# A re-planned start for a tuned RMSNorm and matmul kernel: weights first, two tiles transposed by the DMA crossbar, the next tiles fetched earlier

## The chip, the cores and the metric

One core of one Trainium2 chip. Times are device microseconds (us) of that core; one execution of a kernel is one time. The span is the profile's time from the first to the last instruction, some 2 us less than the measured time. A run and the kernel before are compared on the same chip in the same rounds.

Words used below: SBUF is the on-chip memory of the core, PSUM the one into which TensorE writes. An eviction copies a finished result from PSUM to SBUF. A crossbar transpose is a DMA that reads a tile from SBUF and writes it back transposed. A transfer lands when the profile shows it complete; its time to landing is counted from its issue. The granted clock is the share of its full speed at which TensorE ran, as the profile records it.

## The reference, cut to what matters

```python
# x: (8, 1024, 768), w_qkv: (768, 2304), all float32
rms = np.sqrt(np.mean(x ** 2, axis=-1, keepdims=True) + eps)
return np.matmul(x / rms * gamma, w_qkv)
```

x is 8192 rows, 64 tiles of 128 rows. For each tile the kernel does 6 blocks of K times 2304 columns: 24 matmuls of 512 columns and 6 of 256.

## The kernel before

The whole program is a list of (planned time, operation), sorted by time. Each engine gets its operations in that order and waits, in order, for what each one needs. The first six tiles, "the head", follow a hand-made plan while the weights arrive; from tile 6 on each tile repeats one pattern.

```python
    def load_w(c): ...                       # SyncE: float32 piece of the weights, in 2 KB or 1 KB rows
    def conv(c, ko, eng): ...                # gamma * w -> bf16, on VectorE, ScalarE or GpSimd
    def cast(t, eng="DVE"): ...              # x tile -> bf16
    def tr(t):                               # six transposes on TensorE, into PSUM
        PT[t] = psum.tile([P, KO, P], bf16, name="pm")
        for ko in range(KO):
            nc.tensor.transpose(out=PT[t][:, ko, :], in_=XB[t][:, ko * P:(ko + 1) * P], identity=ident)
    def cp(t, eng): ...                      # PSUM -> xT
    def trans_dma(t):                        # or: one DMA through the crossbar, SBUF to SBUF
        XT[t] = xTp.tile([P, KO, P], bf16, name="xT")
        nc.sync.dma_start_transpose(out=XT[t], in_=XB[t])
    # ... the plan of the head: tiles 0 to 2 transposed in float32, 3 to 5 in bf16, all on TensorE
    for t in range(HEAD, MT):                # from tile 6 on
        at(now - 15, load_x, t)
        at(now - 8.5, cast, t)
        at(now - 7.5, trans_dma, t)
        at(now - 5, stat, t)
        at(now - 3, recip, t)
        for n0 in range(0, N, NT):
            at(now, mm, t, n0, range(KO))    # ... eviction by VectorE and ScalarE in turn, store by SyncE
```

Eight PSUM buffers go round in the order in which they are asked for.

## Time and profile before

| | kernel before |
|---|---|
| time | 389.87 us, median of 3 (389.81 to 390.78) |
| span of the profiled run | 387.9 us |
| first main matmul | 8.48 us |
| tile 6 begins (worked out in the prediction) | 45.28 us |
| last matmul ends | 384.37 us |

The lines of the profile, and the sum made of them, stand in the prediction. The holes below are the time of the head beyond its main matmuls at full clock.

### The profile page before, as it was taken

How to read it: one execution, taken by the hardware profiler on the slowest of the kernel's cores; microseconds unless marked ns; L12 is line 12 of the kernel's file. 1: busy time of each engine (PE TensorE's matmuls, PEld its weight loads, DVE VectorE, ACT ScalarE, POOL GpSimd, SP SyncE). 2: the span in 40 equal slices, each digit the busy share in tenths (PEclk: the TensorE clock that was granted, in tenths of full speed). 3: DMA queues.
4: the chain of work that ended last, by engine and by line, in shares of the span. 5: the costliest groups of instructions: out<-in, count | busy, mean ns of one | idle time of the engine just before them, and what ended most of it. 6: DMA issues, size and time to landing. Idle time of an engine off the chain costs nothing.

```text
span 387.9 us, 5500 instructions
## 1 busy us (share of the span) xinstructions
PE 379.5 (98%) x1953; PEld 194.3 (50%) x1992; DVE 159.1 (41%) x317; ACT 178.1 (46%) x359; POOL 5.9 (2%) x12
## 2 busy tenths in 40 slices
PE   7999999999999999999999999999999999999996
PEld 6444644554554554554554554554554554554553
DVE  3667634343433343433343433343334343334332
ACT  6652234544444544444534444534434535434532
POOL 1310000000000000000000000000000000000000
PEclk9999999999999999999999999999999999999999
DMA  7999999999999999999999999999999999999974
GB/s 272 392 384 358 308 369 284 397 301 274 333 311 305 279 326 295 290 330 300 276 346 288 302 317 280 318 311 304 287 318 301 297 318 303 287 325 292 292 264 189
DMA packets 87606, 119.51 MB, mean 308 GB/s; under 512 B 50710, under 2 KB 59676, under 8 KB 87580
## 3 DMA queue, kind: packets, MB, share of 16 engines
q1 hardware_dynamic: 87568, 119.17, 100.7%
q8 instruction: 15, 0.25, 0.3%
q14 instruction: 11, 0.09, 0.1%
q10 hardware_dynamic: 12, 0.00, 0.0%
HBM read 32.25 MB, written 75.50 MB: 278 GB/s over the span
## 4 chain that ended last, share of the span: by engine, by line
PE 94%; DMA 3%; SPq 1%; issue 1%; DVE 0%; ACT 0%
PE pm L216 94%; DMA w_f<-in_w_qkv_dram 2%; DMA xT<-xb 2%; SPq L140 0%; SPq L145 0%; PE pm L183 0%; DVE w_b L151 0%; ACT ot L232 0%; DVE ot L230 0%
## 5 line engine op out<-in xcount | busy, mean ns | idle before, releaser
L216 PE MATMUL pm<-w_b,xT 128*128 128x512 bf16 (+1 forms) x1881 | 372.4, 357 | 3.0 <-DMA xT<-xb 0.4
L216 PEld LDWEIGHTS <-xT 128*128 128x128 bf16 x1920 | 187.6, 98 | 186.6 <-issue 0.8
L230 DVE TENSOR_SCALAR ot<-pm,rstd 128x512 f32<-128x512 f32 (+1 forms) x168 | 116.7, 696 | 210.3 <-PE pm L216 210.3
L232 ACT ACTIVATE ot<-pm,rstd 128x512 f32<-128x512 f32 (+1 forms) x152 | 97.9, 645 | 187.0 <-PE pm L216 141.7
L170 ACT ACTIVATE sq<-x_t 128x768 bf16<-128x768 f32 x64 | 53.4, 834 | 10.2 <-DMA x_t<-in_x_dram 10.2
L159 DVE CAST xb<-x_t 128x768 bf16<-128x768 f32 x61 | 33.2, 545 | 4.1 <-DMA x_t<-in_x_dram 4.0
L172 ACT ACTIVATE rms<-ssq,eps_sb 128x1 f32<-128x1 f32 x64 | 18.8, 294 | 2.1
L170 ACT ACTIVATION_READ_ACCUMULATOR sq<-x_t 128x1 f32 x64 | 12.2, 191 | 0.0
L177 DVE RECIPROCAL rstd<-rms 128x1 f32<-128x1 f32 x64 | 9.8, 153 | 0.0
L151 DVE TENSOR_SCALAR w_b<-w_f,g_sb 128x512 bf16<-128x512 f32 (+1 forms) x14 | 6.5, 494 | 6.1 <-DMA w_f<-in_w_qkv_dram 6.0
L153 ACT ACTIVATE w_b<-w_f,g_sb 128x512 bf16<-128x512 f32 (+1 forms) x10 | 6.1, 651 | 5.7 <-DMA w_f<-in_w_qkv_dram 5.7
L155 POOL TENSOR_SCALAR w_b<-w_f,g_sb 128x512 bf16<-128x512 f32 (+1 forms) x6 | 5.2, 864 | 23.5 <-DMA w_f<-in_w_qkv_dram 23.5
L265 PE MATMUL pm<-warm 128*128 128x128 bf16 x35 | 3.8, 300 | 1.0 <-DVE eps_sb L124 1.0
L265 PEld LDWEIGHTS <-warm 128*128 128x128 bf16 x35 | 3.5, 142 | 1.0 <-DVE eps_sb L124 1.0
L197 PE MATMUL pm<-ident_f,x_t 128*128 128x128 f32 x18 | 2.8, 292 | 0.8 <-DMA x_t<-in_x_dram 0.8
L197 PEld LDWEIGHTS pm<-ident_f,x_t 128*128 128x128 f32 x18 | 2.2, 155 | 1.1 <-DMA x_t<-in_x_dram 1.0
L127 ACT ACT_TABLE_LOAD x1 | 1.3, 1283 | 1.3 <-PEq L325 1.3
L159 DVE CAST xT<-pm 128x512 bf16<-128x512 f32 (+1 forms) x3 | 1.7, 596 | 0.0
L159 DVE COPY xT<-pm 128x768 bf16<-128x768 bf16 x3 | 1.6, 547 | 0.0
L248 DVE COPY g_sb<-pm 128x6 f32<-128x6 f32 x1 | 0.2, 165 | 3.6 <-PE pm L247 3.6
L183 PEld LDWEIGHTS <-xb 128*128 128x128 bf16 x18 | 1.2, 98 | 0.9 <-DVE xb L159 0.6
L183 PE MATMUL pm<-ident,xb 128*128 128x128 bf16 x18 | 1.5, 220 | 0.0
(13 smaller groups left out, 3.1 us busy)
## 6 DMA issues: line engine op xcount, KB each, us to landing
out_dram<-ot SPq DMA_DIRECT2D x126, 512.0 KB, 4.0
x_t<-in_x_dram SPq DMA_DIRECT2D x64, 384.0 KB, 4.3
out_dram<-ot SPq DMA_DIRECT2D x64, 128.0 KB, 3.2
w_f<-in_w_qkv_dram SPq DMA_DIRECT2D x2, 1536.0 KB, 13.3
w_f<-in_w_qkv_dram SPq DMA_DIRECT2D x3, 768.0 KB, 8.5
w_f<-in_w_qkv_dram SPq DMA_DIRECT2D x6, 256.0 KB, 5.8
out_dram<-ot SPq DMA_DIRECT2D x4, 256.0 KB, 2.0
xT<-xb SPq DMA_TRANSPOSE x58, 4.4
```

Source lines behind the costliest of these rows:

```text
L151: nc.vector.tensor_scalar(out=o, in0=i, scalar1=g, scalar2=None, op0=mult)
L153: nc.scalar.activation(out=o, in_=i, func=AF.Copy, scale=g, bias=0.0)
L155: nc.gpsimd.tensor_scalar(out=o, in0=i, scalar1=g, scalar2=1.0, op0=mult, op1=mult)
L159: nc.vector.tensor_copy(out=out, in_=in_)
L170: nc.scalar.activation(out=sq, in_=X[t], func=AF.Square, accum_out=ssq)
L172: nc.scalar.activation(out=rms, in_=ssq, func=AF.Sqrt, scale=inv_k, bias=eps_sb)
L177: nc.vector.reciprocal(out=r, in_=RS[t])
L197: nc.tensor.transpose(out=PT[t, h][:, ko - k0, :], in_=X[t][:, ko * P:(ko + 1) * P], identity=ident_f)
L216: nc.tensor.matmul(out=PM[t, n0][:, :nl], lhsT=XT[t][:, ko, :], rhs=w_b[:, ko, n0:n0 + nl], start=(b == 1), stop=(b == KO))
L230: nc.vector.tensor_scalar(out=o, in0=pm[:, :nl], scalar1=RS[t], scalar2=None, op0=mult)
L232: nc.scalar.activation(out=o, in_=pm[:, :nl], func=AF.Copy, scale=RS[t], bias=0.0)
L265: nc.tensor.matmul(out=wps, lhsT=warm, rhs=warm, start=True, stop=True)
```

## The change

Its intent is to start the first matmul sooner and to take work off TensorE in the head.

```diff
-ARRIVALS = "xxxwwwxwwwwwxxwww"
+LOADS = [                                   # the first transfer is now two K blocks of weights (512 KB)
+    (-9.00, "w", 0), (-8.99, "x", 0), (-8.98, "x", 1), (-8.97, "x", 2), (-8.96, "w", 1),
+    ... (-8.88, "w", 8), (-8.87, "x", 4), (-8.86, "w", 9), (-8.85, "x", 5), (-8.84, "w", 10),
+    (-8.83, "w", 11), (-8.81, "w", 12), (-8.79, "x", 6), (-8.78, "x", 7),
+]
 HEAD_PLAN = [                               # a new list; cut to the lines of tiles 4 and 5
-    (17.24, "tr", 4), ... (18.02, "cp", 4, "DVE"), (18.23, "tr", 5), ... (20.40, "cp", 5, "DVE"),
+    (18.03, "cast", 4, "DVE"), ... (18.64, "xbar", 4), ... (21.65, "xbar", 5), ...
+    (22.77, "mm", 4, 0, "012345"), ... (27.73, "mm", 5, 0, "012345"), ...
-HEAD_END = 44.51
+HEAD_END = 43.31
-    def trans_dma(t):
+    def xbar(t, engine=nc.scalar):
...
+        ahead = 6.0 if t < HEAD + 5 else 0.0
-        at(now - 15, load_x, t)
-        at(now - 8.5, cast, t)
-        at(now - 7.5, trans_dma, t)
+        if ("x", t) not in {q[1:] for q in LOADS}:
+            at(now - 15 - ahead, load_x, t)
+        at(now - 8.5 - ahead, cast, t)
+        at(now - 7.5 - ahead, xbar, t, nc.sync)
```

The weights come in 13 pieces instead of 11. GpSimd takes 16 of the 30 weight conversions instead of 6, tile 2 is transposed in bf16, and some pools have more buffers.

## The prediction

Cut from the recorded text, where marked: statements on DMA queues and engines that no trace behind the prediction shows.

> **What bounds the kernel now.** I read the page of the profile first, by engine and by the slices of the span, then the chain that ended last, in order of time, then the timeline of the head (everything before tile 6), and last the tiles' own views for weights, x, transposed x and the crossbar. On the page:
>
> ```profile
> PE 379.5 (98%) x1953; PEld 194.3 (50%) x1992; DVE 159.1 (41%) x317; ACT 178.1 (46%) x359; POOL 5.9 (2%) x12
> PE   7999999999999999999999999999999999999996
> PEclk9999999999999999999999999999999999999999
> GB/s 272 392 384 358 308 369 284 397 301 274 333 311 305 279 326 295 290 330 300 276 346 288 302 317 280 318 311 304 287 318 301 297 318 303 287 325 292 292 264 189
> PE pm L216 94%; DMA w_f<-in_w_qkv_dram 2%; DMA xT<-xb 2%; SPq L140 0%; SPq L145 0%; PE pm L183 0%; DVE w_b L151 0%; ACT ot L232 0%; DVE ot L230 0%
> ```
>
> TensorE is busy in every slice but the first and the last, at full granted clock, and 94% of the chain is the main matmul line. Only the ends have slack. The chain in order of time says where:
>
> ```profile
> 4.02 6.60 DMA w_f<-in_w_qkv_dram
> 10.64 0.50 DVE w_b L151
> 11.19 6.80 PE pm L216 x30
> ...
> 45.48 6.04 DMA xT<-xb
> 51.56 6.22 PE pm L216 x31
> ...
> 384.37 0.47 ACT ot L232
> ```
>
> So there are two places where something other than TensorE sets the pace: the weight loads before 11.19 us, and a crossbar transpose, issued at 45.48, that landed just when a tile was to start. After 51.56 us I find no wait at all: 57 tiles take 384.37 - 51.56 = 332.81 us, 5.839 us each (0.2163 us per 512 columns). 64 tiles of that are 373.7 us, a floor the change does not touch: the multiplications are the same. From the timeline:
>
> ```profile
> 3.85 0.84 ACT L170 ACTIVATE sq<-x_t 128x768 bf16<-128x768 f32 x1 [1.01 <-DMA x_t<-in_x_dram]
> 6.93 0.64 PEld L197 LDWEIGHTS pm<-ident_f,x_t 128*128 128x128 f32 x6 [1.04 <-DMA x_t<-in_x_dram]
> 8.48 2.10 PE L216 MATMUL pm<-w_b,xT 128*128 128x512 bf16 x8 [0.39 <-POOL w_b L155]
> 51.56 10.76 PE L216 MATMUL pm<-w_b,xT 128*128 128x512 bf16 x51 [0.44 <-DMA xT<-xb]
> ```
>
> The first x tile was there at 3.85, the third at 6.93, the first real matmul ran at 8.48. The head has six tiles, 6 x 5.839 = 35.03 us of matmul. Tile 7 was ready to start 0.44 before 51.56, so tile 6 began at 51.56 - 0.44 - 5.84 = 45.28. The head's holes are then 45.28 - 8.48 - 35.03 = 1.77 us. In all: 8.48 start + 35.03 + 1.77 holes + 338.66 for 58 tiles + 0.44 wait + 3.5 tail (384.37 to 387.9) = 387.9. What a change of the head can take from is 8.48 + 1.77 + 0.44 = 10.7 us, under 3% of the whole, and most of the 8.48 is the latency of first loads. The measured time is 389.87, so 1.97 us lie outside the span; I keep that.
>
> [...] from 18 to 30 us the 16 engines already moved 386 GB/s, so transposes on the ScalarE queue take their share of it from weights. [...] No ScalarE-queue transfer of size is in this trace[...]. [...] the same GpSimd conversion of 512 columns took 0.69 us alone at 7.74 and 0.99 at 14.09 while VectorE converted.
>
> **The change part by part.** The weights' views and those of x give the arrivals now; I add up the kilobytes in issue order and read a time for each sum.
>
> ```profile
> 6.92 0.84 ACT L170 ACTIVATE sq<-x_t 128x768 bf16<-128x768 f32 x1 [1.03 <-DMA x_t<-in_x_dram]
> 8.32 0.49 DVE L151 TENSOR_SCALAR w_b<-w_f,g_sb 128x512 bf16<-128x512 f32 x1 [1.35 <-DMA w_f<-in_w_qkv_dram]
> 14.03 0.72 ACT L153 ACTIVATE w_b<-w_f,g_sb 128x512 bf16<-128x512 f32 x1 [1.25 <-DMA w_f<-in_w_qkv_dram]
> 18.03 0.56 DVE L159 CAST xb<-x_t 128x768 bf16<-128x768 f32 x1 [0.44 <-DMA x_t<-in_x_dram]
> ```
>
> That is 1152 KB at 6.92, 1664 at 8.32, 3840 at 14.03, 5376 at 18.03: about 384 KB per us after the start. The plan of the kernel before had these at 6.44, 7.81, 13.47, 17.47: reality lags the plan by half a us. I assume the same for the new plan.
>
> 1. *Start.* Two K blocks first (512 KB), then x0, x1, x2. By my sums w0 lands at 4.5, x0 (896 KB) at 5.8, x1 (1280 KB) near 7.2. New TensorE order puts the six float transposes of tile 1 ahead of the first matmul; six took 0.88 us (6.94 to 7.82). So the first matmul is at 7.2 + 0.9 = 8.1, against 8.48: gain 0.4, not the 0.67 between the plans (8.02 to 7.35).
> 2. *Tile 2 in bf16.* It now waits for x2 (1664 KB, 8.3), a cast of 0.56, six transposes of 0.34 to 0.5: 9.3. Tile 0's two matmuls end at 8.55, so a hole of 0.75 us. From there the new plan's 8.27 stands at 9.3, a lag of 1.0, and TensorE's plan is closed up, so the lag stays.
> 3. *Tiles 4 and 5 by crossbar.* It takes 12 transposes and two copies of 0.55 us out. On TensorE each group of six cost a hole of 0.34 to 0.4 (17.82 to 18.20, 18.85 to 19.18): gain 0.7. Added are two issues on ScalarE. From the view of the transposing line:
>
> ```profile
> L206 SPq DMA_TRANSPOSE xT<-xb x58: 1272/1563/2548, 38.4 to 370.8; - x58
> DMA to landing us min/median/max: 3.2/4.4/6.9
> ```
>
>    so 1.3 to 2.5 us of ScalarE's queue each (hidden: its next work for TensorE is not due for 6 us), and landing 3.2 to 6.9 us after issue. x4 (5760 KB) lands at 19.0, cast until 19.6, issue at 19.65, landing at 24.05 with the median, 26.5 at worst. TensorE wants tile 4 at plan 22.77 + lag 1.1 = 23.9. Stall 0.15 to 2.6, chosen 0.3[...]. Tile 5 is wanted at 27.73 + 1.4 and lands near 27.8: no stall.
> 4. *More GpSimd conversions*, 16 instead of 6, at up to 0.98 us. Blocks 5 to 8 make a chain from 13.4 to 19.3; each one ends within 0.1 us of TensorE's need at that lag. I take 0.1.
> 5. *Next tiles fetched ahead of head stores.* x6 and x7 are queued behind the last weights, cast and transposed 6 us earlier. The cause of the 0.44 wait was that SyncE issued tile 7's transpose only after a store that waited for an eviction (45.33, then 45.48). Gone: gain 0.44. The early cast may hold VectorE for about 2 us until x6 lands (about 31); eviction buffers have several us of room then, so nothing.
>
> The sum: 8.1 + 35.03 + holes (0.75 tile 2, 0.45 tile 3, 0.3 tile 4, 0.1 GpSimd, 0.15 rest = 1.75) = 44.9 for tile 6, against 45.28; + 338.66 + 3.5 = 387.05 of span, + 1.97 = **389.0 us**.
>
> **Rivals.** *The schedule holds as written*: tile 6 starts 44.51 - 43.31 = 1.2 us earlier, plus 0.44: 388.2. For it: the plan before was off by a nearly constant lag. Against it: x1 and x2 arrive later than before. *The crossbar becomes the wait*: in the busy stretch of 36 to 62 us it landed in 5.5 to 6.9 us (the view of transposed x), not in the 4.1 that the plan allows (18.64 to 22.77). Then TensorE stands some 1.5 to 2.5 us at tile 4, in place of 0.7 saved: 390.3 to 390.9. For it: at 19.6 the engines are full with weights[...]. *The prefetch disturbs what follows*: VectorE held by the early cast, or x and transposes crowding the stores, so that a wait comes near tile 6 or 11, where the 6 us lead ends: about 390. Against: between 38.0 and 45.3 us the DMA moved only 246 GB/s, there is room. *Nothing matters*: start gained and tile 2's hole cancel, 389.5.
>
> **Range and chances.** All rivals lie within 1.7 us of 389.0. Range 387.9 to 390.6 for 8 in 10. Two per cent are 7.8 us; the sum available is 10.7 and mostly latency, and a loss of that size needs a stall an order above the ones found. Faster 0.01, same 0.98, slower 0.01.
>
> **What would show it.** In the changed profile: first main matmul near 8.1 (right if 7.8 to 8.4); a hole of TensorE near 8.6 to 9.3 before tile 2's transposes; a wait on transposed x near 24 (0 to 0.5; over 1.5 proves the crossbar rival); tile 6 at 44.9; no wait near 50; 5.839 us per tile from there. The prediction is wrong if the ScalarE-queue transpose lands in over 5 us, if the arrivals change with the order by more than I assume, or if the DMA-heavy stretch after the head makes TensorE wait where it does not now.

## The result, and the profile after

The changed kernel takes 396.15 us (median of 4, 395.14 to 397.03), the kernel before in the same rounds 389.84. The ratio is 1.0157, 95% interval 1.0127 to 1.0187. (A ratio is the mean time of one kernel's runs over that of the other's in the same rounds, so it is not quite the ratio of the medians.) It is slower by 6.3 us, inside 2%, and outside the stated range.

The page of the changed kernel, busy times, slices of the span and chain:

```profile
PE 380.8 (97%) x1947; PEld 194.1 (49%) x1985; DVE 155.9 (40%) x311; ACT 175.4 (45%) x353; POOL 12.5 (3%) x22
PE   8949999999999999999999999999999999999996
PEclk9998999999999999999999999999999999999999
PE pm L231 91%; DMA x_t<-in_x_dram 3%; DMA xT<-xb 2%; DMA w_f<-in_w_qkv_dram 1%; SPq L155 0%; SPq L160 0%; DVE xb L174 0%; ACT ot L247 0%; DVE ot L245 0%
```

The third slice of TensorE is 4 where it was 9, and the fourth digit of the granted clock fell from 9 to 8. In these two rows only TensorE's first slice changed besides, from 7 to 8. The chain in order of time (start, length, what):

```profile
9.25 10.92 DMA x_t<-in_x_dram
20.20 0.56 DVE xb L174
20.79 8.89 DMA xT<-xb
29.73 8.08 PE pm L231 x30
...
390.36 0.47 ACT ot L247
```

Tile 4's x was asked for at 9.25 us and was there at 20.2; VectorE cast it; ScalarE issued the crossbar transpose at 20.79; it landed 8.89 us later, and TensorE started at once. TensorE's own timeline, with the idle time before each group in brackets:

```profile
7.73 0.60 PE L231 MATMUL pm<-w_b,xT 128*128 128x512 bf16 x2
20.32 4.38 PE L231 MATMUL pm<-w_b,xT 128*128 128x512 bf16 x19 [0.85 <-POOL w_b L170]
29.73 30.58 PE L231 MATMUL pm<-w_b,xT 128*128 128x512 bf16 x153 [5.04 <-DMA xT<-xb]
```

The first matmul came sooner than before (7.73 against 8.48). Then TensorE stood for 5.04 us before tile 4 (by the profile's modelled end of the matmul before). The wait has a second cost, which the weight loads behind it show, one for each matmul:

```profile
30.14 0.15 PEld L231 LDWEIGHTS <-xT 128*128 128x128 bf16 x1 [0.28 <-issue]
30.56 0.15 PEld L231 LDWEIGHTS <-xT 128*128 128x128 bf16 x1 [0.28 <-issue]
32.27 0.15 PEld L231 LDWEIGHTS <-xT 128*128 128x128 bf16 x1 [0.28 <-issue]
32.69 3.12 PEld L231 LDWEIGHTS <-xT 128*128 128x128 bf16 x15 [0.27 <-issue]
```

They are 0.42 us apart until 32.69, then 0.21: seven matmuls at half speed, about 1.5 us, and the granted clock between 29.7 and 33 us was 0.55. Among the experiments, a wait of 3.88 us (e6) had the same effect (weight loads 0.43 us apart up to 31.12) and one of 2.32 us (e2) did not (no matmul up to 34 us took over 0.38 us, against 0.63 in the changed kernel and in e6).

**The sum.** Counting back from the last matmul, tile 6 began at 390.36 - 58 x 5.839 = 51.70 us. The head's holes were 51.70 - 7.73 - 35.03 = 8.94 us, against 1.77. The span grew by 6.1 us: 7.17 of holes, less 0.75 of earlier start, less the 0.44 us wait at tile 7, which is gone, plus 0.1 of tail. Of the 8.94 us, 5.30 lie between the end of the matmul before tile 4 (20.32 + 19 x 0.2163 = 24.43) and 29.73, about 1.5 are the slow clock, and the rest are the holes at tiles 2 and 3 (0.69 and 0.47) and a wait on a GpSimd conversion (0.85 in the profile, 1.05 by counting matmuls).

### The profile page after: what moved, and what is told of

Its sections match the earlier page's. It is cut to its first block, busy times and chain, and to the rows that moved or that the text cites. A ratio compares the mean times of both kernels' runs of the same rounds, so it can differ in the third digit from the quotient of the medians.

```text
span 394.0 us, 5493 instructions
## 1 busy us (share of the span) xinstructions
PE 380.8 (97%) x1947; PEld 194.1 (49%) x1985; DVE 155.9 (40%) x311; ACT 175.4 (45%) x353; POOL 12.5 (3%) x22
## 4 chain that ended last, share of the span: by engine, by line
PE 91%; DMA 7%; SPq 1%; issue 1%; DVE 0%; ACT 0%
PE pm L231 91%; DMA x_t<-in_x_dram 3%; DMA xT<-xb 2%; DMA w_f<-in_w_qkv_dram 1%; SPq L155 0%; SPq L160 0%; DVE xb L174 0%; ACT ot L247 0%; DVE ot L245 0%
## 5 line engine op out<-in xcount | busy, mean ns | idle before, releaser
L174 DVE CAST xb<-x_t 128x768 bf16<-128x768 f32 x62 | 34.0, 548 | 5.1 <-DMA x_t<-in_x_dram 5.1
L170 POOL TENSOR_SCALAR w_b<-w_f,g_sb 128x512 bf16<-128x512 f32 (+1 forms) x16 | 11.8, 751 | 19.5 <-DMA w_f<-in_w_qkv_dram 19.5
L168 ACT ACTIVATE w_b<-w_f,g_sb 128x512 bf16<-128x512 f32 (+1 forms) x6 | 3.7, 644 | 5.3 <-DMA w_f<-in_w_qkv_dram 5.3
L166 DVE TENSOR_SCALAR w_b<-w_f,g_sb 128x512 bf16<-128x512 f32 (+1 forms) x8 | 3.5, 433 | 4.4 <-DMA w_f<-in_w_qkv_dram 4.3
L212 PE MATMUL pm<-ident_f,x_t 128*128 128x128 f32 x12 | 1.8, 282 | 0.4 <-DMA x_t<-in_x_dram 0.3
L212 PEld LDWEIGHTS pm<-ident_f,x_t 128*128 128x128 f32 x12 | 1.3, 141 | 0.8 <-DMA x_t<-in_x_dram 0.8
L176 ACT CAST xT<-pm 128x512 bf16<-128x512 f32 x2 | 1.1, 575 | 0.2 <-PE pm L212 0.2
```

The lines of the kernel that those rows point to most:

```text
L166: nc.vector.tensor_scalar(out=o, in0=i, scalar1=g, scalar2=None, op0=mult)
L168: nc.scalar.activation(out=o, in_=i, func=AF.Copy, scale=g, bias=0.0)
L170: nc.gpsimd.tensor_scalar(out=o, in0=i, scalar1=g, scalar2=1.0, op0=mult, op1=mult)
L174: nc.vector.tensor_copy(out=out, in_=in_)
L212: nc.tensor.transpose(out=PT[t, h][:, ko - k0, :], in_=X[t][:, ko * P:(ko + 1) * P], identity=ident_f)
```

## The experiments

**Theory.** The crossbar transposes on ScalarE's queue share the 16 DMA engines with the loads that SyncE has already queued, and get a small part of them (13.9% of their time, against 95.3% for SyncE's queue, from 20.8 to 29.5 us in the changed kernel). That makes them late, and this alone is the loss. **Rivals:** the ScalarE queue or its issue is slow in itself; the new order of loads brings x and weights too late whatever does the transposing; the earlier fetch of tiles 6 and 7 crowds the head.

### e1: tiles 4 and 5 on TensorE again

```diff
-    (18.64, "xbar", 4), ... (21.65, "xbar", 5),
+    (21.68, "tr", 4), (21.80, "cp", 4, "DVE"), ... (24.05, "tr", 5), ... (24.15, "cp", 5, "DVE"),
-    (25.36, "mm", 4, 1024, "012"), ... (27.08, "mm", 4, 1024, "345"), (27.73, "mm", 5, 0, "012345"),
+    (27.08, "mm", 5, 0, "012345"), (28.37, "mm", 4, 1024, "012345"),
```

Tile 4's third accumulator moved because the two transposes take two more turns of the PSUM buffers.

> The new head with one part undone: tiles 4 and 5 are transposed on TensorE and copied by VectorE, as before; to keep the rotation of PSUM buffers free of a deadlock, tile 4's third accumulator is moved behind tile 5's first. If the late crossbar transpose carries the whole loss, the 5.0 us wait and the slow clock after it vanish: first matmul at 7.7, holes of 0.9 (tile 2), 0.5 (tile 3), 1.3 (GpSimd conversion), 0.4 + 0.4 (tiles 4, 5), tile 6 at about 46.2, 390.3 us. If instead tile 4's late arrival (x4 at 20.2) or the weights are the cause, TensorE still stands for several us before tile 4 and the time stays at 394 or more.

Measured: 389.59 us (389.38 to 389.77), ratio 0.9993 (0.9979 to 1.0008) to the kernel before. TensorE's waits from its first main matmul on:

```profile
PE pm L231 <- POOL w_b L170: 0.3, 1, 0.3
PE pm L231 <- DVE xT L174: 0.2, 1, 0.2
PE pm L198 <- DVE xb L174: 0.2, 1, 0.2
```

The wait of 5 us is gone and so is the loss. The new order of loads is not at fault: in this run x4's cast started at 19.48, within a microsecond of the changed kernel's, and TensorE did not wait for it. The two transposes, with their gaps, cost TensorE about 0.35 us each; tile 4 also waited 0.20 us for their copy. The start gained 0.91 us (7.57 against 8.48), but tile 6 begins at 384.03 - 338.66 = 45.37, so the holes are 2.77 us against 1.77: they take that gain back.

### e2: the same transposes, with the competing loads held back

```diff
-    (-8.84, "w", 10), (-8.83, "w", 11), (-8.81, "w", 12), (-8.79, "x", 6), (-8.78, "x", 7),
+    (21.66, "w", 10), (21.661, "w", 11), (21.662, "w", 12), (21.663, "x", 6), (21.664, "x", 7),
+    (21.655, "gate", 5)     # SyncE copies 8 KB out of tile 5's xT, so it waits until that has landed
```

> The changed kernel, but the loads of the last three weight pieces and of tiles 6 and 7 are held back on SyncE until tile 5's transpose has landed (a small copy out of it is the gate). Theory of shared engines (small crossbar packets take turns with the big packets queued by SyncE): with the traffic gone by about 23.2 us, tile 4 lands about 4.5 us after issue instead of 8.9, tile 5 about 4 instead of 11.8, TensorE's wait falls from 5.0 to under 1, time about 390.5 us. Rival, the ScalarE queue is slow in itself: 8.9 us again and 396 us or more.

Measured: 393.8 us (393.26 to 394.11), ratio 1.0100. The landing of the two transposes, and what TensorE waited for:

```profile
DMA to landing us min/median/max: 2.8/2.9/3.0
```
```profile
PE pm L235 <- DVE ot L249: 2.3, 1, 2.3
PE pm L235 <- DMA xT<-xb: 1.5, 2, 1.0
```

From the same queue and the same engine, the same transposes land in 3.0 and 2.8 us instead of 8.9 and 11.8. So the ScalarE queue is not slow in itself, and the traffic beside it is the cause. (The second one's 11.8 us hold one thing more: at its issue, 24.08, the first, in the same queue, was still 5.6 us from landing.) TensorE did not wait for tile 4 or 5 at all. The time was not 390.5 as expected, because the cure has a price: the DMA engines moved only 106 GB/s from 20 to 25 us and 100 from 25 to 29.7 (e1: 384 in both), so the weights came late; VectorE, in order, stood before a conversion, an eviction came late (the 2.3 us), and later transposes were late (the 1.5 us, after 58 us).

### e3: TensorE kept busy through the wait

```diff
+    (22.765, "idle", 80),        # 80 idle 128x128 matmuls
     (22.77, "mm", 4, 0, "012345"),
```

> The changed kernel with 80 idle 128x128 matmuls ahead of tile 4's first matmul, so that TensorE works through the wait. If the wait itself costs 5.0 us and the lowered clock after it (mean 0.82 over 29.7 to 38 us) about 1.0 to 1.5 us more, the clock stays at 1.00 and the time falls by 1.0 to 1.5 us, to about 394.9. If the low clock costs nothing the time stays within 0.3 us of 396.15.

Measured: 395.44 us (395.33 to 397.49), ratio 1.0161 (1.0129 to 1.0192). TensorE:

```profile
24.21 4.63 PE L280 MATMUL pm<-warm 128*128 128x128 bf16 x80
29.29 5.14 PE L231 MATMUL pm<-w_b,xT 128*128 128x512 bf16 x23 [0.45 <-DMA xT<-xb]
35.50 24.83 PE L231 MATMUL pm<-w_b,xT 128*128 128x512 bf16 x135 [1.07 <-DMA xT<-xb]
```

The clock stayed at 1.00, as expected, but the expected gain of 1.0 to 1.5 us did not come: the median is 0.7 us lower, within the spread, and the ratio to the kernel before is the same (1.0161 and 1.0157). The last line tells why: the faster TensorE reached tile 5 before its transpose (issued at 23.76, landed 11.7 us later) and waited 1.07 us there. In the changed kernel tile 5 landed at 35.9, just as the slower TensorE came to it (its weight load waited 0.15 us at 35.96). So the slow clock is real, but most of what it cost would have been spent waiting for the second late transpose.

### e4: the two transposes from SyncE

```diff
-    def xbar(t, engine=nc.scalar):
+    def xbar(t, engine=nc.sync):
```

> The changed kernel with the two head transposes issued from SyncE instead of ScalarE, at the same place in the program. SyncE reaches them only behind the last loads (about 23.2 us). If its queue is served in order, they land behind tile 7, at about 32 us: a wait of 7 to 8 us, some 399 us. If the ScalarE queue is the slow thing, they land about 4.4 us after issue as all SyncE transposes do, at 27.6, and the time is about 394.

Measured: 398.56 us (398.31 to 398.86), ratio 1.0224. The chain:

```profile
23.07 9.00 DMA xT<-xb
32.07 0.05 issue
32.12 8.04 PE pm L231 x28
```

SyncE came to the transpose 2.3 us later than ScalarE had, behind its last loads, and it landed after 9.00 us, at 32.07, where the first reading of e4 (about 32 us) put it. The change's choice of ScalarE was the better of the two by 2.4 us of time; it gained the earlier issue. It did not gain a faster transfer: 8.89 against 9.00 us.

### e6: the competing weights in rows of half the size

```diff
+        for m in ((0, 256), (256, 512)) if c in (9, 10, 11) else ((0, n),):
+            nc.sync.dma_start(out=WF[c][:, :, m[0]:m[1]], in_=wv[:, k0:k1, n0 + m[0]:n0 + m[1]])
```

> The changed kernel with the competing weights in smaller packets: pieces 9, 10 and 11 are each loaded by two DMAs of 1 KB rows instead of one of 2 KB rows, the same bytes in the same order. If the crossbar's small packets take turns with the other queue's packets one for so many, each turn is now about half as long: tile 4 lands in about 5.5 to 6.5 us instead of 8.9 and the time falls by some 2 to 3 us. If the landing is set by bytes in flight, it stays at 8.9 and the time at 396.

Measured: 395.2 us (394.91 to 396.2), ratio 1.0143. Tile 4 landed in 7.9 us, tile 5 in 10.9. That is a miss for both readings. The queues from 20.8 to 29.5 us (q1 is SyncE's queue, q10 ScalarE's: packets, MB, share of the 16 engines), first the changed kernel, then e6:

```profile
q1 hardware_dynamic: 1723, 2.77, 95.3%
q10 hardware_dynamic: 856, 0.21, 13.9%
```
```profile
q1 hardware_dynamic: 2254, 2.27, 96.0%
q10 hardware_dynamic: 813, 0.20, 17.5%
```

These averages (2.0 packets of SyncE's queue for one of the crossbar's in the changed kernel, 2.8 in e6; 0.21 of 2.98 MB, 7%, for the transposes) mix two stretches. The same view of the changed kernel from 20.8 to 24.8 us, where there is no line for q10 at all, and from 25 to 28 us:

```profile
q1 hardware_dynamic: 788, 1.54, 103.9%
```
```profile
q1 hardware_dynamic: 673, 0.72, 84.2%
q10 hardware_dynamic: 669, 0.17, 32.2%
```

First stretch: the transpose was issued at 20.79, and its first packet moved at 24.88, 4.1 us later (1.2 us in e2). It was 4.1 us in e3 and e8 too, and 4.4 in e6. Before that packet SyncE's queue passed 1.58 MB (e3 1.59, e8 1.54, e6 1.56), whether in 814 packets or, in e6, in 1517. So in these four runs the data that went first agreed within 3%, and the packets did not, as the second reading of e6 had it.

Second stretch: the two queues moved nearly equal numbers of packets (673 to 669, e3 680 to 677, e8 651 to 647, from 25 to 28 us). In the changed kernel the crossbar's were of about 256 bytes (0.17 MB in 669), SyncE's of 1.07 KB on average (0.72 MB in 673), and tile 4 landed 4.8 us after its first packet, instead of 1.7 in e2. In e6 the bulk went fast (756 packets from 25.0 to 26.5), with only 0.15 MB of SyncE's beside them, but the last ones came near 28.5. Neither reading foresaw both parts. Why some 1.6 MB went first, and why e6's last packets were late, no run shows.

### e8: the crossbar part alone, in the kernel before

```diff
-    (17.24, "tr", 4), ... (18.02, "cp", 4, "DVE"), (18.23, "tr", 5), ... (20.40, "cp", 5, "DVE"),
+    (16.48, "xbar", 4), ... (17.48, "xbar", 5),       # on the ScalarE queue
```

> The kernel before with the crossbar part alone: tiles 4 and 5 transposed through the ScalarE queue, everything else unchanged. Tile 4 issued near 17.6 with weights in flight until 29, landing 8 to 9 us later near 26.3, wanted near 20: a wait of some 6 us, and tile 5 perhaps 1.5 more, time about 396.5. If the new order of loads were what makes the transposes slow, they would land in 4 to 5 us here and the time would be about 391.

Measured: 400.38 us (399.5 to 400.72), ratio 1.0266. Tile 4's transpose was issued at 18.73 and TensorE started on it at 28.22, after a wait of 7.25 us; tile 5's took 12.8 us:

```profile
28.22 32.14 PE L216 MATMUL pm<-w_b,xT 128*128 128x512 bf16 x151 [7.25 <-DMA xT<-xb]
```

The loss comes with this part in the old order of loads too, and is larger there, because the old plan wants tile 4 sooner. The expected size was too small by 4 us. The expectation left out the slow clock: the twelve matmuls after the wait stood 0.43 us apart (granted clock 0.52 from 28.2 to 33.6 us), which is about 2.5 us. The wait was 7.25 us where some 6 were expected, the first matmul came at 9.15 (8.48 in the kernel before), and tile 7 waited 0.73 us for its own transpose (issued at 55.58), where the kernel before had 0.44.

### e5: the earlier fetch alone, in the kernel before

```diff
+        ahead = 6.0 if t < HEAD + 5 else 0.0
+        at(-7.0 + 0.1 * t if t < HEAD + 2 else now - 15 - ahead, load_x, t)
+        at(now - 8.5 - ahead, cast, t)
+        at(now - 7.5 - ahead, trans_dma, t)
```

> The kernel before with the third part alone: tiles 6 and 7 loaded behind the last weights, casts and transposes of tiles 6 to 10 planned 6 us earlier. The prediction's step says the 0.44 us wait on tile 7's transpose goes and nothing takes its place: 389.4 us, a ratio of about 0.999. If the prefetch crowds the head (weights or stores later), the time rises by 0.5 us or more.

Measured: 389.44 us (389.07 to 389.62), ratio 0.9987 (0.9975 to 1.0000). After 19.72 us TensorE has no wait:

```profile
19.72 40.58 PE L216 MATMUL pm<-w_b,xT 128*128 128x512 bf16 x207
```

This part does what it was meant to, and what the prediction said of it: the wait at tile 7 is gone. In time the gain is small, and its interval ends at 1.0000.

### e7 and e9: what is left of the change without the crossbar

e7 is e1 with TensorE taking the eighth piece in the order 2, 1, 0, and ScalarE copying tile 4's transposes. e9 is e7 with one more conversion moved off GpSimd.

```diff
-    (18.67, "mm", 0, 1024, "012"), ... (21.80, "cp", 4, "DVE"),
+    (18.67, "mm", 0, 1024, "210"), ... (21.80, "cp", 4, "ACT"),      # e7, so for tiles 0 to 3
-    (21.00, "conv", 9, 3, "POOL"),
+    (21.00, "conv", 9, 3, "ACT"),                                    # e9
```

> The kernel of e1 with two small mends: TensorE takes the eighth piece's blocks in the order 2, 1, 0, so that the slow GpSimd conversion of block 0 is wanted last (the wait of 0.35 us goes), and ScalarE copies tile 4's transposes (the wait of 0.2 us behind a cast goes). Expected 389.0 us, ratio 0.998 to the kernel before; if a new wait appears there, 389.6 as e1.

> The kernel of e7 with one conversion of the ninth piece (block 3) moved from GpSimd to ScalarE, idle there from 20.9 us. The 0.29 us wait on GpSimd at 22.4 us goes: 389.1 us, ratio 0.998. If another wait takes its place, 389.4 as e7.

Measured: e7 389.39 us (389.0 to 389.72), ratio 0.9986 (0.9973 to 0.9998); e9 389.45 us (389.12 to 389.62), ratio 0.9985 (0.9969 to 1.0001). In e7 the wait of 0.35 us on GpSimd went and one of 0.29 us on GpSimd came at 22.44; in e9 it was 0.40 us at 22.75. So e9's wait did not go as expected, and e7 missed its 389.0. e7 beats the changed kernel clearly and the kernel before by about 0.14%, at the edge of the noise (e5's and e9's intervals reach 1.0000 and 1.0001). In e7 the start gained 0.72 us and the fetch 0.44, but tile 6 begins at 383.80 - 338.66 = 45.14, so the holes of the head are 2.35 us against 1.77.

## Why the prediction was wrong

The step that failed is in part 3: "Stall 0.15 to 2.6, chosen 0.3". The choice rested on the assumption that a transpose on a separate queue does not wait for the queued weights. The stall was 5.30 us: 1.58 MB of SyncE's data went first (20.79 to 24.88 us), and then, from 25 to 28 us, 669 packets of the transposes moved beside 673 of SyncE's.

| step | predicted | measured |
|---|---|---|
| first matmul | 8.1 us | 7.73 |
| hole before tile 2's transposes | 0.75 | 0.7 (8.16 to 8.85; both counted over 2 and 13 matmuls of 0.2163) |
| hole at tile 3 | 0.45 | 0.47 |
| wait on GpSimd conversion | 0.1 | 0.85 (0.28 to 0.71 in e1 to e4) |
| landing of tile 4's transpose | 4.4 after 19.65 | 8.89 after 20.79 |
| stall at tile 4 | 0.3 | 5.30 |
| clock after it | not considered | about 1.5 |
| wait at tile 7 | gone | gone |
| tile 6 begins | 44.9 | 51.70 |

1. *Landing.* 4.4 us was the median of 58 transposes on SyncE's queue, nearly all of them in the steady part. The worst, 6.9, came from the head's end. None of them ran beside as many queued weights. The assumption on the other queue is what failed: the transpose was issued among the weights, but 4.1 us passed before its first packet moved (1.2 in quiet), and the rest moved beside SyncE's larger packets (1.07 KB against 256 bytes, see e6). The landing goes from 2.8 to 3.0 us in quiet (e2) to 8.9, or 11.8 for the second (changed kernel). The median of a transfer's landing was taken as its cost; it is the cost at that row's traffic. The prediction had named the sign of this: it is wrong "if the ScalarE-queue transpose lands in over 5 us".
2. *The rival.* "The crossbar becomes the wait" named the mechanism, but was sized from the same view (5.5 to 6.9), at 390.3 to 390.9. ("All rivals lie within 1.7 us of 389.0" is a slip: 390.9 is 1.9 away and above the range, and the worst landing of part 3, with its stall of 2.6, would give 391.3.) It also left out the slow clock after a long wait, about 1.5 us here.
3. *Arrival.* x4 was cast at 20.20, 1.2 us after the 19.0 worked out from the kernel before; this falls straight into the stall. The stall came out some 5.1 us above the 0.15 of the prediction's own sum: 4.5 are the landing, 1.1 the arrival, less 0.5 by which TensorE itself came later (24.43 against 23.9). The arrival is partly chance: with the same loads up to there the cast began at 19.48 in e1, and the transpose was issued at 20.26 in e2 and 20.48 in e3.
4. *What was right.* The 5.839 us per tile and the tail held; the fetch ahead removed the wait that its step names (e5: 0.13%, 0.5 us, at the edge of the noise); the start gained more than said, 0.75 us. The holes at tiles 2 and 3 were right to 0.1 us. The wait on GpSimd was sized too small by 0.75 us in the profiled run, less in others. Without the crossbar (e1) the sum is 389.6, inside the predicted range.

What stays open: why some 1.6 MB of the other queue went before a crossbar packet moved (1.54 to 1.59 in four runs, see e6); how much the slow clock would cost if the second transpose were in time (e3 could not separate them); and how long a wait brings the slow clock: its record falls to half at about 29.25 us in the changed kernel, 4.55 us after the last matmul's modelled end, but in e8 at 23.2 us, 2.2 us after it (no matmul ran just then to confirm it).

## What to carry to other kernels

A transfer's time to landing is no property of the transfer: for a crossbar transpose of 128 x 768 bf16 it was 2.8 to 3.0 us in quiet (e2), 4.4 (median, from SyncE) in the kernel before, 7.9 (e6) to 9.4 (e8) for the first one on ScalarE's queue beside queued loads, and up to 12.8 (e8) for the second. Read it where the same queues are as full as they will be, and if no such row exists, widen the range upward. Issuing a small-packet DMA such as a crossbar transpose from a second queue while another queue has megabytes waiting made it land sooner here (29.7 us against 32.1 in e4), yet not soon (8.89 us after its issue); work that TensorE wants within a few microseconds was cheaper at 0.35 us of TensorE (e1) than in such a queue (5.04 us of wait). Where a wait of some 4 us is possible on TensorE, add the slow clock after it to the cost: matmuls at half speed followed a wait of 3.88 us here (e6), and none followed one of 2.32 (e2). An average over a window can hide two regimes: read the queues in shorter windows before inferring a rule.
